# ReLU and row sum of 32 x 512 x 1024: who waits for the last store, and what closes the program

## Chip, core and metric

One core of a Trainium2 chip runs the kernel. The metric is the time of one execution on the device, in microseconds (us). Five engines have instruction streams of their own and meet only at semaphores: PE (TensorE), ACT (ScalarE), DVE (VectorE), POOL (GpSimd) and SP (SyncE). SP computes nothing here; it issues the transfers and waits.

## What is computed

```python
def reference(x):                      # x: 32 x 512 x 1024, float32
    relu_x = np.maximum(x, 0)
    return np.sum(relu_x, axis=-1)     # 32 x 512, float32
```

There are 16,384 rows of 1024 numbers. Each is clamped at zero and summed. 67.1 MB are read and 64 KB are written.

## The kernel before

**Tiling.** The 128 partitions hold 128 rows at a time, so each partition has 128 rows to sum. They come in seven blocks of 16 rows per partition (8 MB a block, `TWO`, `ACT`, `DVE`, lines 14 to 16) in three buffers `io`, and an eighth block that arrives in shrinking pieces: 8, 4, 2 and 1 rows (`TAIL`, line 18), and then the last row in four column pieces of 244 to 268 numbers (`PIECES`, line 19).

**Work on a block.** In the first six blocks ACT clamps groups of rows in place (`clamp`, line 112), and DVE sums them (`total`, line 120). In the sixth block ACT also does two rows by itself (`act_row`, line 127: clamp and sum in one instruction). The seventh block is shared row by row: nine rows on ACT and seven on DVE (`dve_row`, line 137). The eighth is shared in turns. The sums stand in one tile, `res`. The last row's four parts are summed on DVE one after the other; the last of them (line 205) also adds in the three sums before it.

**Transfers.** All transfers are issued on SP: 15 loads (line 94) and three stores of `res` (line 105). The first load is moved ahead of the program's opening barrier (`issue_ahead_of_the_barrier`, `EARLY`). A load into a used buffer waits until DVE is done with the block that was in it. The third store, 1 KB, holds the last two rows of each partition and waits for the last DVE instruction (lines 104, 105, 215). Every store adds 16 to the semaphore `stored` when it lands, so all three have landed when it is 48.

**Order and semaphores.** Nothing is scheduled by the framework: each engine runs its instructions in the order of the code, and semaphores are written by hand (`Semaphores`, line 47). There are 18 of them, which the trace numbers 99 to 116; 116 is `stored`.

**The opening barrier.** The framework opens the program with an all-engine barrier (line 259 in the profile). ACT, DVE, PE and SP each run a drain that adds one to a gather semaphore (96), then an event instruction that waits for a release semaphore (97) and takes one from it. POOL runs a drain, an event that waits until 96 is 4 and takes 4 off, and an event that adds 4 to 97. The trace of before has a record of each of these instructions.

**The closing block.** The framework also makes a closing block. As it makes it, it holds this, in order: a drain on SP; an all-engine barrier of the same 11 instructions as the opening one; on POOL a drain and a range clear that sets semaphores 99 to 116 to zero; and a second all-engine barrier of 11 instructions. The kernel before empties this block (line 41) and puts three things in: on POOL a wait for `stored` (line 42), POOL's drain of the clear, and the range clear (`semaphore_clear`, line 219, returns these two). In the trace the wait is not an instruction of its own: POOL's drain at line 29 carries it. PE, ACT, DVE and SP have nothing in the block.

**After the kernel** the runtime runs its own closing barriers and clears; they carry no line of the kernel and are not in the span, but the trace has their semaphore updates. [...]

Of the kernel before, what the change touches and what calls it, by code (L numbers as in the profile page):

```python
# [23 lines left out]
def kernel(tc: tile.TileContext, x: bass.AP, out: bass.AP):  # L24
    nc = tc.nc
    sems = Semaphores(tc)

    tc.close()
    tc.compile()
    nc.cur_bb = nc.bb_map[tc.start_bb_name]  # L30
    body = nc.cur_bb.bb.instructions
    ends = list(body)
    body.clear()
    n_stores = relu_sum(nc, sems, x, out)
    body.extend(ends)


    nc.cur_bb = nc.bb_map[tc.start_bb_name + "_end"]
    body = nc.cur_bb.bb.instructions
    clear = semaphore_clear(body)  # L40
    body.clear()
    nc.gpsimd.wait_ge(sems.stored, 16 * n_stores)
    body.extend(clear)
    issue_ahead_of_the_barrier(tc, EARLY)


# [169 lines left out]
    return n_store  # L216


def semaphore_clear(instructions):

    pool = [i for i in instructions if i.engine == mybir.EngineType.Pool]
    at = next(
        n for n, i in enumerate(pool) if getattr(i, "is_reset_sema", False)
    )
    return pool[at : at + 2]


def issue_ahead_of_the_barrier(tc: tile.TileContext, n_loads: int):


    SP = mybir.EngineType.SP
    blocks = tc.nc.main_func.blocks
    opening = blocks[0].instructions
    body = next(b for b in blocks if b.name == tc.start_bb_name).instructions
    loads = [i for i in body if i.engine == SP][:n_loads]
    for i in loads:
        assert isinstance(i, mybir.InstDMACopy)
        body.remove(i)
    at = next(
        n  # L240
        for n, i in enumerate(opening)
        if i.engine == SP and isinstance(i, mybir.InstDrain)
    )
    opening[at:at] = loads
# [30 lines left out]
```

## Time and profile before

| | us |
|---|---|
| median of 3 runs (161.95, 162.01, 162.01) | 162.01 |
| the profiled execution's own time | 161.95 |
| its span, from the kernel's first instruction to its last | 160.064 |
| lies around the span | 1.89 |
| DVE busy | 117.7 (74%) |
| ACT busy | 104.2 (65%) |
| POOL busy | 0.2 |
| mean rate of the transfers over the span | 420 GB/s |

Times in the profile count from the start of the span. A view prints microseconds with two digits or fewer; the trace under it has nanoseconds for the start and length of every instruction, and the time of every semaphore update. A letter q behind an engine (SPq, POOLq) stands for its sequencer: waits, drains, events and the issue of a transfer are not counted as busy time, but they have records. A record starts when the instruction's wait is over, so a wait is seen as the gap in front of it.

### The profile page before, as it was taken

The page shows a single profiled execution, that of the slowest core. Times are in us where ns is not written, and L with a number is a line of the kernel's source. Part 1 is how long each engine was busy: PE and PEld are TensorE (multiplying, and loading weights), DVE is VectorE, ACT ScalarE, POOL GpSimd, SP SyncE. Part 2 cuts the span into 40 slices and gives each one's busy share as a digit, 9 for nine tenths or more (in the row PEclk, how much of TensorE's full clock was granted, in tenths as well). Part 3 has the DMA queues.
Part 4 walks back from the last instruction along what each step waited for, and adds up shares of the span by engine and source line. Part 5 has one row for each costly group of instructions (what it writes and reads, how often), then busy time and mean ns, then how long its engine had stood idle before and what let it go on. Part 6 is the DMA issues. An engine that isn't in the chain of part 4 may idle for free.

```text
span 160.1 us, 133 instructions
## 1 busy us (share of the span) xinstructions
DVE 117.7 (74%) x43; ACT 104.2 (65%) x50; POOL 0.2 (0%) x4
## 2 busy tenths in 40 slices
DVE  0000000009999499994999999999999999999994
ACT  3000059990799708995099942999239992599993
POOL 0000000000000000000000000000000000000000
DMA  7996996996996996997998999979969969999993
GB/s 262 524 524 262 524 524 262 524 524 262 524 508 278 524 508 278 524 475 311 524 409 377 524 393 393 524 328 459 524 278 508 524 262 524 393 393 422 409 400 96
DMA packets 2592, 67.18 MB, mean 420 GB/s; under 512 B 672, under 2 KB 1184, under 8 KB 1312
## 3 DMA queue, kind: packets, MB, share of 16 engines
q1 hardware_dynamic: 2592, 67.18, 98.0%
HBM read 67.11 MB, written 0.07 MB: 420 GB/s over the span
## 4 chain that ended last, share of the span: by engine, by line
DMA 43%; DVE 33%; ACT 17%; another core or an unknown queue 3%; SPq 1%; issue 0%
DVE res L120 32%; DMA io<-in_x_dram 25%; DMA piece<-in_x_dram 18%; ACT io L112 17%; SPq L94 1%; DVE piece L137 1%; DVE piece L205 0%
## 5 line engine op out<-in xcount | busy, mean ns | idle before, releaser
L120 DVE TENSOR_REDUCE res<-io 128x8 f32<-128x8192 f32 (+2 forms) x9 | 101.1, 11287 | 40.0 <-ACT io L112 40.0
L112 ACT ACTIVATE io<-io 128x8192 f32<-128x8192 f32 (+2 forms) x9 | 81.7, 9110 | 47.1 <-DMA io<-in_x_dram 47.1
L127 ACT ACTIVATE io<-io 128x1024 f32<-128x1024 f32 x20 | 20.9, 1043 | 5.4 <-DMA io<-in_x_dram 5.3
L137 DVE TENSOR_SCALAR_CACHE_REDUCE io<-io 128x1024 f32<-128x1024 f32 x13 | 15.0, 1214 | 0.2
L127 ACT ACTIVATION_READ_ACCUMULATOR io<-io 128x1 f32 x20 | 3.7, 187 | 0.0
L112 ACT ACT_TABLE_LOAD x1 | 1.3, 1283 | 0.8 <-PEq L259 0.8
L137 DVE TENSOR_SCALAR_CACHE_REDUCE piece<-piece 128x244 f32<-128x244 f32 (+2 forms) x3 | 1.2, 416 | 0.4 <-DMA piece<-in_x_dram 0.4
L137 DVE DVE_READ_ACCUMULATOR io<-io 128x1 f32 x13 | 1.1, 82 | 0.0
L205 DVE TENSOR_SCALAR_CACHE_REDUCE piece<-piece 128x271 f32<-128x271 f32 x1 | 0.4, 435 | 0.0
L137 DVE DVE_READ_ACCUMULATOR piece<-piece 128x1 f32 x3 | 0.3, 84 | 0.0
L259 POOL MEMSET const-bfloat16-1.0<- 128x1 bf16 x1 | 0.1, 101 | 0.0
L259 POOL MEMSET const-uint8-127<- 128x1 uint8 x1 | 0.1, 101 | 0.0
L259 POOL MEMSET const-float32-0.0<- 128x1 f32 x1 | 0.1, 98 | 0.2 <-issue 0.2
L259 POOL MEMSET const-float32-1.0<- 128x1 f32 x1 | 0.1, 98 | 0.0
L205 DVE DVE_READ_ACCUMULATOR piece<-piece 128x1 f32 x1 | 0.1, 82 | 0.0
## 6 DMA issues: line engine op xcount, KB each, us to landing
io<-in_x_dram SPq DMA_DIRECT2D x1, 4096.0 KB, 21.6
io<-in_x_dram SPq DMA_DIRECT2D x1, 2048.0 KB, 26.1
io<-in_x_dram SPq DMA_DIRECT2D x1, 1024.0 KB, 28.1
io<-in_x_dram SPq DMA_DIRECT2D x1, 512.0 KB, 28.9
piece<-in_x_dram SPq DMA_DIRECT2D x1, 134.0 KB, 28.5
piece<-in_x_dram SPq DMA_DIRECT2D x1, 130.0 KB, 28.6
piece<-in_x_dram SPq DMA_DIRECT2D x1, 126.0 KB, 28.7
piece<-in_x_dram SPq DMA_DIRECT2D x1, 122.0 KB, 28.8
```

Of the source, the lines that this page charges most:

```text
L94: dma = nc.sync.dma_start(out=dst, in_=src)
L112: i = nc.scalar.activation(out=ap, in_=ap, func=RELU)
L120: nc.vector.tensor_reduce(out=res[:, m : m + n], in_=ap, axis=mybir.AxisListType.X, op=ADD).wait_op(sems.act, n_act, "sem-ge").then_inc(se ...
L127: i = nc.scalar.activation(out=ap, in_=ap, func=RELU, accum_out=res[:, m : m + 1])
L137: i = nc.vector.tensor_scalar(out=ap, in0=ap, scalar1=0.0, scalar2=None, op0=MAX, op1=ADD, accum_out=accum_out,)
L205: nc.vector.tensor_scalar(out=last[:, :], in0=last[:, :], scalar1=0.0, scalar2=None, op0=MAX, op1=ADD, accum_out=res[:, NT - 1 : NT],).wai ...
L259: nc = _bacc.Bacc("TRN2", target_bir_lowering=False, num_devices=1)
```

## The change

The closing block is no longer cut down. It keeps all that the framework put there, and a wait for `stored` on SP is put in front of it. The function that picked POOL's two instructions is gone.

```diff
     nc.cur_bb = nc.bb_map[tc.start_bb_name + "_end"]
     body = nc.cur_bb.bb.instructions
-    clear = semaphore_clear(body)
+    ends = list(body)
     body.clear()
-    nc.gpsimd.wait_ge(sems.stored, 16 * n_stores)
-    body.extend(clear)
+    nc.sync.wait_ge(sems.stored, 16 * n_stores)
+    body.extend(ends)
     issue_ahead_of_the_barrier(tc, EARLY)
...
-def semaphore_clear(instructions):
-
-    pool = [i for i in instructions if i.engine == mybir.EngineType.Pool]
-    at = next(
-        n for n, i in enumerate(pool) if getattr(i, "is_reset_sema", False)
-    )
-    return pool[at : at + 2]
```

The closing block then reads, engine by engine:

```text
SP     [wait stored >= 48] drain; drain, 96 += 1; wait 97 >= 1, 97 -= 1; drain, 96 += 1; wait 97 >= 1, 97 -= 1
ACT, DVE, PE                      drain, 96 += 1; wait 97 >= 1, 97 -= 1; drain, 96 += 1; wait 97 >= 1, 97 -= 1
POOL   drain; wait 96 >= 4, 96 -= 4; 97 += 4; drain; clear 99..116; drain; wait 96 >= 4, 96 -= 4; 97 += 4
```

Each drain that adds to 96 also waits until 97 is 0. Loads, compute and stores are the same in both kernels.

## Prediction

> **What bounds the kernel now.** I read the page's head and chain first, to see what sets the end.
>
> ```profile
> span 160.1 us, 133 instructions
> ...
> DMA 43%; DVE 33%; ACT 17%; another core or an unknown queue 3%; SPq 1%; issue 0%
> ```
>
> The loads and the compute fed by them make the time, and the diff touches none of them. So only the part behind the last sum can move. Next, the chain in order of time and the timeline of the last 2 us (start, length, what):
>
> ```profile
> 127.86 28.83 DMA piece<-in_x_dram
> 156.69 0.02 issue
> 156.72 1.18 DVE piece L137 x6
> 157.90 0.03 issue
> 157.92 0.44 DVE piece L205 x2
> ```
>
> ```profile
> 158.28 0.08 DVE L205 DVE_READ_ACCUMULATOR piece<-piece 128x1 f32 x1
> 158.39 0.33 SPq L105 DMA_DIRECT2D out_dram<-res  x1
> ```
>
> The chain view stops at the last compute instruction, DVE's at 158.36, yet the span runs to 160.06. The 1.70 us between are the last store and what waits for it. The instructions of line 29 (POOL's closing ones) are seen only when that line is asked for:
>
> ```profile
> L29 POOLq DRAIN  x1: 88/88/88, 159.8 to 159.8; - x1
> L29 POOLq EVENT_SEMAPHORE_RANGE_CLEAR  x1: 136/136/136, 159.9 to 159.9; - x1
> ```
>
> In nanoseconds: the store is issued from 158.394, its last landing is at 159.787, POOL's drain starts at 159.811 (0.024 later), and the clear ends at 160.064, the end of the span. From the drain's start to the clear's end it is 0.088 + 0.029 gap + 0.136 = **0.253 us**. This stretch is on the path, and here the change puts its instructions.
>
> **Behind the span.** The trace's updates of semaphore 2 show the runtime's closing chain: 1.003, 157.597, 160.590, 160.634, 160.657, 160.754, 160.794, 160.828, 160.874. Its gaps tell who is who. PE left the opening barrier at 0.771 and adds first (0.232 later); ACT's last instruction ends at 157.489 and it adds second (0.108 later); the third update has to be POOL's, since DVE (158.36) and SP (158.73) were done long before: it comes 0.526 after the clear. The rest follows in hops of 0.023 to 0.097. So POOL, and POOL alone, holds back the end of the program now: what moves the end of POOL's work moves the time by as much, unless another engine becomes later in this chain.
>
> **The price list.** The barrier that the change adds twice at the end has already run once, at the opening (line 259; smallest/median/largest ns, first to last start):
>
> ```profile
> L259 POOLq EVENT_SEMAPHORE  x2: 17/17/17, 0.6 to 0.7; - x2
> L259 DVEq DRAIN  x1: 10/10/10, 0.1 to 0.1; - x1
> L259 ACTq DRAIN  x1: 8/8/8, 0.1 to 0.1; - x1
> ...
> L259 POOLq DRAIN  x1: 179/179/179, 0.3 to 0.3; - x1
> L259 PEldq DRAIN  x1: 8/8/8, 0.3 to 0.3; - x1
> ...
> L259 SPq DRAIN  x1: 132/132/132, 0.4 to 0.4; - x1
> ...
> L259 PEldq EVENT_SEMAPHORE  x1: 51/51/51, 0.7 to 0.7; - x1
> ```
>
> In nanoseconds, SP arrives last: a transfer's issue ends 0.049 before its drain, the drain runs 0.431 to 0.563, POOL's two events start at 0.589 and 0.667, the second ends at 0.684, and the four engines' events start at 0.709 to 0.720. PE's is the last to end, at 0.771.
>
> **The change, step by step, from the moment `stored` is 48.**
>
> 1. The wait moves from POOL to SP. Nothing is queued behind it but SP's closing instructions, for which the barrier waits. POOL started 0.024 after the last landing; SP's last issue started 0.017 after the DVE update that it waited for (158.377 to 158.394). I take no difference: 0.00.
> 2. SP's two drains. SP's only drain took 0.132, just after an issue; those of ACT, PE and DVE took 0.008 to 0.010. Here the first comes 1.0 us after SP's last issue and the second right after another drain. I take SP's own row for the first and DVE's for the second, with the gap of 0.049: 0.132 + 0.049 + 0.010 = **0.191** (ends: 0.046 with 0.008 twice and a gap of 0.03; 0.313 with 0.132 twice).
> 3. The first barrier's end, from the end of SP's drain to the end of POOL's release: 0.684 - 0.563 = **0.121**. ACT, DVE, PE and POOL come to it early (the latest, DVE, is done at 158.36, 1.4 us before), so their drains cost nothing; were SP not last, DVE's would cost 0.010.
> 4. POOL's clear drain and clear: a gap of 0.029 before, then the 0.253 that before pays too: **0.282**. The four engines leave the first barrier and arrive at the second meanwhile: out within 0.087 of POOL's release by the opening's rows, plus a drain of 0.008 to 0.132. That is 0.22 at most against 0.282, so POOL's clear hides it by 0.06; an engine that came later than that would add what it exceeds.
> 5. The second barrier on POOL: gap 0.029, drain 0.088 (line 29's row; ends 0.008 and 0.179), gap 0.029, then from event to event 0.078 and the last event's 0.017: **0.241**.
>
> Sum: 0.191 + 0.121 + 0.282 + 0.241 = 0.835 against 0.253 before, so POOL ends **0.58 us later**. The span grows by some 0.09 more, since PE's last event ends 0.087 after POOL's; the time doesn't, because PE has that much slack in the runtime's chain: its first hop would come 0.087 + 0.232 behind POOL's release, and two hops of 0.035 and 0.038 (the same hops of the runtime's last chain, 161.704, 161.738, 161.776) make it 0.39, while POOL itself takes 0.526.
>
> The profiled execution took 161.95, so the change makes it 161.95 + 0.58 = 162.53. The median of the runs shown is 0.06 above this execution; for the median I forecast **162.59**.
>
> [...] The runtime's own chain that runs last takes 162.061 - 161.704 = 0.357 here, from first update to last. [...]
>
> **Rivals.**
>
> *The tail is hidden (not slower).* POOL's 0.526 between the clear and its update in the runtime's chain is far more than PE's 0.232 or ACT's 0.108. If it belongs to the clear and runs on beside later instructions, the second barrier lies under it. It can shrink only until PE's and ACT's part of the chain is last: PE's release ends 0.087 after POOL's, then a tail like ACT's 0.108, then 0.073 of hops, 0.268 in all. From a POOL tail under 0.27 on, the saving is 0.526 - 0.268 = 0.26, and the change costs 0.58 - 0.26 = 0.32: 162.27, within 0.2%. For it: POOL's tail is the odd one out, and only POOL ran a clear. Against it: the clears are recorded as updates of 99 to 116 at 159.949 to 160.036, before the record ends, so nothing is seen to run on; and if POOL's sequencer is what is busy, the drain behind the clear has to wait for it just as well, which leaves the sum as it is.
>
> *The gaps are dearer.* No row shows POOL going from an event to a drain or from a clear to a drain. If these three gaps are like the 0.078 between its events (+0.15), both SP drains take 0.132 (+0.12), POOL's drain takes the opening's 0.179 (+0.09), and the wait stands by itself as an event on SP (0.017 and a gap of 0.045, +0.06), it is 0.58 + 0.42 = 1.00: 161.95 + 1.00 + 0.06 = 163.01. For it: drains differ by a factor of 20 between engines here. Against it: they all have to go this way.
>
> *The change doesn't do what it says.* The time could stay at 162.01 if the runtime's chain, not the kernel's end, were the limit. The updates speak against that: third to seventh come in hops right behind POOL.
>
> **Numbers.** Forecast (0.45 to 0.80 more) 0.73; dear gaps (above that) 0.13; hidden tail 0.11; nothing, or a gain by something that no row shows, 0.03 (0.01 and 0.02). About 0.2% (0.32 us) is what a measurement of this kernel can tell from no change. Slower by more 0.86, within it 0.12, faster 0.02. The range takes in the hidden tail's 162.27 with some of the cheap drains (step 2 at its low end is 0.145 less, so 162.13 with both; I stop at 162.20) and ends at the dear case's 163.0.
>
> **What the trace would show.** Step 1: SP's first drain starts within 0.03 of the last landing. Steps 2 to 5: some 23 instructions more in the closing block, with SP's two drains summing to about 0.14, POOL's clear some 0.34 later behind the landing than now, and POOL's last event 0.58 later. The span is near 160.73. In semaphore 2 the first three updates stand close together, with the third still some 0.5 behind POOL's release; if it stands at 0.27, the hidden tail was right. I'm wrong if the last load or the last sum moves, or if an engine other than SP arrives last at the first barrier.

## The result, and the profile after

| | before | changed kernel |
|---|---|---|
| median | 161.98 us (4 runs, 161.94 to 162.01) | 162.59 us (4 runs, 162.49 to 162.68) |
| ratio | 1 | 1.0038, 95% interval 1.0020 to 1.0055 |
| profiled execution: time, span | 161.95, 160.064 | 162.68, 160.736 |
| instructions in the profile | 133 | 156 |

The change makes the kernel slower by 0.61 us. The forecast was 162.59.

The page's head and chain of the changed kernel:

```profile
span 160.7 us, 156 instructions
...
DMA 43%; DVE 33%; ACT 17%; another core or an unknown queue 3%; SPq 1%; issue 0%; DVEq 0%
```

The shares are those of before: loads and compute still make the time. The timeline of its last microseconds (start, length, what):

```profile
158.06 0.43 DVE L204 TENSOR_SCALAR_CACHE_REDUCE piece<-piece 128x271 f32<-128x271 f32 x1
158.43 0.08 DVE L204 DVE_READ_ACCUMULATOR piece<-piece 128x1 f32 x1
158.54 0.33 SPq L104 DMA_DIRECT2D out_dram<-res  x1
```

The last sum and the last store are as before, but 0.14 later. The rest is in the closing block, line 29 of the changed kernel (smallest/median/largest ns, first to last start):

```profile
L29 POOLq EVENT_SEMAPHORE  x4: 17/17/17, 160.0 to 160.6; - x4
L29 POOLq DRAIN  x3: 34/41/82, 0.7 to 160.5; - x3
L29 SPq DRAIN  x3: 7/7/7, 160.0 to 160.3; - x3
L29 PEldq DRAIN  x2: 8/8/8, 0.9 to 160.3; - x2
L29 ACTq DRAIN  x2: 14/595/1176, 156.5 to 160.3; - x2
...
L29 PEldq EVENT_SEMAPHORE  x2: 51/51/51, 160.2 to 160.7; - x2
L29 POOLq EVENT_SEMAPHORE_RANGE_CLEAR  x1: 136/136/136, 160.3 to 160.3; - x1
```

Two things are to be seen here. First, 23 more records, as the diff says. Second, SP's drains take 0.007 us each, not the 0.132 of the opening. ACT's first drain is 1.176 long, but it starts at 156.496, under ACT's own last instructions, and ends at 157.672, 2.26 ahead of the last landing; it costs nothing on the path.

The path in nanoseconds, from the record starts and ends of the trace: last landing 159.936; SP's drain with the wait 159.952; SP's second drain ends 160.014; POOL's release of the first barrier ends 160.135; POOL's clear drain runs 160.199 to 160.281, the clear 160.310 to 160.446; POOL's second release ends 160.648; PE's last event ends 160.736. The updates of semaphore 2 behind the kernel start at 160.971, 161.005, 161.210 (POOL's) and 161.254.

An update has a semaphore and a time in the trace, and neither an engine nor a line; "the runtime's" stands for what comes behind the kernel's last instruction, and the engines are read from the times. As in before, the first update of the closing chain comes some 0.23 behind PE's last event (0.235) and the third some 0.5 behind POOL's last instruction (0.562). Nine more updates of semaphore 2 follow in both profiles, the last chain: in before at 161.704, 161.738, 161.776, 161.820, 161.844, 161.942, 161.980, 162.014 and 162.061, in the changed kernel at 162.281, 162.316, 162.354, 162.398, 162.421, 162.520, 162.558, 162.714 and 162.761. A step is the time from one update to the next and is numbered by the update that it ends with.

I cut the end of every profiled execution into three stretches: K (the kernel's) from the last landing to the end of POOL's last instruction; P (POOL's tail) from there to POOL's update of semaphore 2; R (the rest) from that update to the end of the time. The trace marks neither end of the measured time; I count it from the start of the span, so R holds all of the time that lies outside the span behind that update or ahead of the first instruction, and a part of R that no update shows can't be placed. What comes ahead of the last landing is left out, since the landing itself moves between executions (159.68 to 159.99 in the profiles of this study). Differences are against before.

| | K | P | R | K+P+R less before's | change of the medians |
|---|---|---|---|---|---|
| before | 0.277 | 0.526 | 1.360 | 0 | 0 |
| changed kernel | 0.712 | 0.562 | 1.470 | +0.58 | +0.61 |

### The profile page after: what moved, and what is told of

The parts are those of the page before. It is cut to its first block, busy times and chain, and to the rows that moved or that the text cites. A ratio compares the mean times of both kernels' runs of the same rounds, so it can differ in the third digit from the quotient of the medians.

```text
span 160.7 us, 156 instructions
## 1 busy us (share of the span) xinstructions
DVE 117.7 (73%) x43; ACT 104.2 (65%) x50; POOL 0.2 (0%) x4
## 4 chain that ended last, share of the span: by engine, by line
DMA 43%; DVE 33%; ACT 17%; another core or an unknown queue 3%; SPq 1%; issue 0%; DVEq 0%
DVE res L119 32%; DMA io<-in_x_dram 25%; DMA piece<-in_x_dram 18%; ACT io L111 17%; SPq L93 1%; DVE piece L136 1%; DVE piece L204 0%; DVEq L29 0%
```

## The experiments

Theory A is the prediction's: only what stands behind the last landing on POOL's path, and what its tail and the runtime add to it, costs time. The rivals are that the longer program also delays the transfers (B), that POOL's tail belongs to the clear and hides later work (C), and, found on the way, that the number of instructions in the block lengthens the runtime's closing wherever they run (D).

**1. The changed kernel once more.** No edit.

> The changed kernel once more, unchanged, to see what of its 0.61 us is the same in every execution. In its first profile POOL's work behind the last landing took 0.44 us more than before, its tail 0.04 more, and the last landing itself came 0.15 later because one of the 16 DMA engines started its first load 0.30 late. Theory A (the closing block is all of the cost; the late engine is chance): the closing block from SP's drain to POOL's last event is again 0.70 us, but the last landing of the first load moves between profiles, and the time is 0.48 over before, with single runs 0.1 to either side. Theory B (the longer program also delays the transfers): the first load's last landing is again near 21.99 and the time is 0.61 over before.

Measured: 162.57 against 162.02, ratio 1.0035 (1.0023 to 1.0048). The first load's last landing came at 21.783 (21.992 in the first profile, 21.821 in before), the last store's at 159.792. So the late landing was chance, and theory B falls. What makes a landing late isn't shown, and the late start that the expectation names isn't shown to do it: the last of the first load's 16 first packets started at 1.405 in before, at 1.897 in the first profile and at 2.041 here, and here the landing was early. Stretches K and P are the same to the nanosecond, 0.712 and 0.562, and R is 1.474. The first profile's time holds 0.15 of chance, the median 162.59 less of it.

**2. The first barrier alone.** In this and the next three, `first`, `clear` and `second` are the closing block's 12, 2 and 11 instructions, as in experiments 10 and 11; the lines that split it are left out.

```diff
-    body.extend(ends)
+    body.extend(first + clear)
```

> SP waits, then the first barrier and POOL's clear; the second barrier is left out. Theory A (each instruction on POOL's path adds its own time): 0.06 for SP's drains, 0.12 to POOL's release, 0.31 to the clear's end, against 0.25 before: 0.24 us over before. Theory C (POOL's 0.53 us between its last instruction and its step in the runtime's chain belongs to the clear and can run beside a barrier): here nothing follows the clear, so 0.24 as well, and all of the rest is in the second barrier, which would then cost little.

Measured: 162.51 against 162.02, ratio 1.0030 (1.0019 to 1.0042): 0.49, twice the 0.24 expected. Its line 29:

```profile
L29 POOLq DRAIN  x2: 41/62/82, 0.7 to 160.2; - x2
L29 SPq DRAIN  x2: 7/7/7, 159.9 to 160.0; - x2
L29 POOLq EVENT_SEMAPHORE  x2: 17/17/17, 160.0 to 160.1; - x2
...
L29 POOLq EVENT_SEMAPHORE_RANGE_CLEAR  x1: 136/136/136, 160.3 to 160.3; - x1
```

The kernel's part is as theory A has it: K is 0.510, 0.233 over before, and P is 0.526. The other 0.24 is in R, 1.595, outside the kernel's span (0.17 on average over all six runs, see the table at the end).

**3. The second barrier alone.** POOL waits and clears as before.

```diff
-    nc.sync.wait_ge(sems.stored, 16 * n_stores)
-    body.extend(ends)
+    nc.gpsimd.wait_ge(sems.stored, 16 * n_stores)
+    body.extend(clear + second)
```

> POOL waits for the stores and clears as before; behind it the second barrier alone. Theory A: 0.20 us of POOL's drain and two events, and a tail 0.04 longer: 0.24 over before. Theory C: the barrier lies in POOL's tail, at most 0.05 over before. A third reading, that the cost is the wait's move to SP and the first barrier: 0.00 here.

Measured: 162.45 against 162.02, ratio 1.0029 (1.0019 to 1.0040): 0.43. K is 0.480 (+0.20), P 0.561 (+0.035), R 1.595 (+0.24). The barrier isn't hidden in POOL's tail; the tail comes whole behind it, and theory C falls here. R is again 0.24 longer in the profile (0.18 on average over eight runs). Two drains of line 29 are worth a look:

```profile
L29 POOLq DRAIN  x2: 34/61/88, 159.9 to 160.2; - x2
...
L29 SPq DRAIN  x1: 129/129/129, 158.9 to 158.9; - x1
```

POOL's drain behind the clear takes 0.034, and SP's, which here comes 0.05 behind the issue of the last store, takes 0.129.

**4. Both barriers, the wait on POOL between them.**

```diff
-    nc.sync.wait_ge(sems.stored, 16 * n_stores)
-    body.extend(ends)
+    body.extend(first)
+    nc.gpsimd.wait_ge(sems.stored, 16 * n_stores)
+    body.extend(clear + second)
```

> Both barriers stay, but the wait for the stores is on POOL behind the first barrier, so all engines pass the first barrier while the last store is under way. Theory A (only what stands behind the wait costs): the same as with the second barrier alone, 0.24 over before. If instead the number of barriers or instructions costs, wherever they stand: 0.48 as in the changed kernel.

Measured: 162.41 against 162.02, ratio 1.0024 (1.0012 to 1.0036): 0.39. K is 0.474 (+0.20) and P 0.561, as with the second barrier alone: the first barrier, done by 159.29 while the store was under way, costs nothing there (K was 0.480 without it). R is 1.468, which is the changed kernel's and not that of the two kernels with one barrier.

So R depends on something that the kernels with both barriers share. In their traces the eighth of the nine steps in the runtime's last chain takes 0.16 where before has 0.034, and the time ends 0.08 ahead of the last update; in before it ends 0.11 ahead of it; in the two kernels with one barrier the chain is as in before, but the time ends 0.12 behind the last update. So of R's growth the updates show 0.08 with both barriers and nothing with one; the 0.23 there may lie behind the last update or ahead of the span.

**5. Both barriers ahead of the wait.**

```diff
-    nc.sync.wait_ge(sems.stored, 16 * n_stores)
-    body.extend(ends)
+    body.extend(first + second)
+    nc.gpsimd.wait_ge(sems.stored, 16 * n_stores)
+    body.extend(clear)
```

> Both barriers stand ahead of POOL's wait for the stores, so all their instructions run while the last store is under way; behind the wait there are POOL's drain and clear alone, as before. It has the changed kernel's instructions but for the engine that waits. In the runs so far the closing block on POOL grew by 0.20 to 0.44 us, while the times grew by 0.39 to 0.55: some 0.1 to 0.2 us come behind the kernel, in the runtime's own closing. Theory A (only the path behind the last landing costs): same as before, within 0.1. Theory D (more instructions in the block, wherever they run, lengthen the runtime's closing by 0.1 to 0.2 us): 0.1 to 0.2 over before.

Measured: 162.17 against 162.08, ratio 1.0007 (0.9998 to 1.0016). K is 0.270 and P 0.527, as before. Its line 29 shows the second barrier over before the store had landed (last landing 159.832):

```profile
L29 POOLq EVENT_SEMAPHORE  x4: 17/17/17, 159.0 to 159.4; - x4
L29 POOLq DRAIN  x3: 34/41/82, 0.7 to 159.9; - x3
...
L29 PEldq EVENT_SEMAPHORE  x2: 51/51/51, 159.2 to 159.5; - x2
L29 POOLq EVENT_SEMAPHORE_RANGE_CLEAR  x1: 136/136/136, 160.0 to 160.0; - x1
```

R is nevertheless 1.481, with the eighth step at 0.166. The median can't tell this 0.12 from nothing, but the trace can: the step is slow although every barrier was long over. So can the time less the span, which is 0.11 longer on average (11 runs against 27 of before, standard error 0.01). That speaks for theory D.

**6. The kernel before, as an experiment.** No edit.

> The kernel before, unchanged, measured as if it were a changed one, for a second profile of it and for what an equal kernel gives: 0.00 with an interval of some 0.1% to either side, single runs 0.1 to 0.2 apart, the first load's last landing anywhere from 21.8 to 22.0, and behind the clear the same 0.526 on POOL and 0.36 in the runtime's last chain.

Measured: 162.06 against 162.08, ratio 1.0003 (0.9992 to 1.0015). K, P and R are 0.276, 0.527 and 1.352. Single runs of before lie between 161.84 and 162.76 in this study, but these stretches repeat within 0.01 in the two profiles.

**7. Four more instructions on ACT.** Against before; the drains run when ACT is done, and nothing waits for them.

```diff
+    for engine, n in [("scalar", 4)]:
+        for _ in range(n):
+            getattr(nc, engine).drain()
     nc.gpsimd.wait_ge(sems.stored, 16 * n_stores)
```

> The kernel before with four more drains on ACT in the closing block; they run at 157.5 us, while DVE and the stores are at work. The changed kernel has four more instructions on ACT than before. With both barriers, even when both ran early, the eighth step of the runtime's last chain took 0.16 us instead of 0.03, the pause before that chain 0.79 instead of 0.83, and the time stood 0.03 further from the last update: 0.11 us in all, all behind the kernel. Theory D (the runtime's closing follows the kernel's instructions in each engine's stream, and the step that is late is ACT's, so four more on ACT alone do it): hop 0.16 and 0.1 over before. If another engine's added instructions do it, or the barriers' waits and not their number: hop 0.034 and the time of before.

Measured: 162.10 against 162.00, ratio 1.0009 (1.0000 to 1.0017). Where the drains ran:

```profile
L44 ACTq DRAIN  x4: 8/11/1176, 156.3 to 157.6; - x4
```

They are over 2 us ahead of the last landing, and K and P are before's (0.276, 0.527). The eighth step of the last chain takes 0.166 and R is 1.520, 0.16 more. Theory D with ACT as the engine foretold it. Which engine makes the eighth step isn't shown.

**8. Two more on ACT.**

```diff
+    for engine, n in [("scalar", 2)]:
```

> The same with two drains on ACT, as many instructions as one barrier adds there. With one barrier the runtime's chains were as before, but the time stood 0.12 behind the last update instead of 0.11 ahead of it: 0.23 more. Theory D with ACT as the engine: no slow hop, the time 0.12 behind the last update and 0.23 over before. Otherwise as before.

Measured: 162.26 against 162.00, ratio 1.0017 (1.0008 to 1.0025). The eighth step is 0.035, and the time ends 0.11 behind the last update: R is 1.575, 0.22 more, as expected. None of this 0.22 is between two updates, so the trace doesn't place it. In these two profiles two instructions more cost more than four; over 11 runs each it is 0.19 against 0.16, with standard errors of 0.02 and 0.01, so that order isn't shown.

**9. The other engines' added instructions, without ACT's.**

```diff
+    for engine, n in [("tensor", 4), ("vector", 4), ("sync", 5), ("gpsimd", 6)]:
```

> The kernel before with the changed kernel's number of instructions on every engine but ACT: four drains more on PE, four on DVE, five on SP, six on POOL, all run ahead of the last landing (POOL's ahead of its wait). Theory D with ACT as the engine: as before, hop 0.034. If the number of instructions on another engine does it: hop 0.16 and 0.1 over before. If neither this nor the four on ACT does it, the cause isn't the number of instructions.

Measured: 162.00 against 162.00, ratio 1.0000 (0.9992 to 1.0009). The eighth step is 0.034. R is 1.312, 0.05 under before: the pause ahead of the last chain is 0.787 instead of 0.830, which the changed kernel shows as well (0.785). With the 0.16 of the four on ACT this makes 0.11, the changed kernel's growth of R to a hundredth.

**10. POOL waits and doesn't clear.** Against before; the range clear is left out.

```diff
-    body.extend(clear)
+    body.extend(clear[:1])
```

> As before, but POOL only waits for the stores with its drain; the range clear is left out, so the kernel leaves its semaphores as they are to the runtime's own closing, whose updates of 99 to 116 are in every trace. Theory A: 0.029 and 0.136 less on POOL, its tail stays at 0.53: 0.17 under before. Theory C (the tail belongs to the clear): tail 0.3 or less, 0.4 or more under before.

Measured: 161.91 against 162.08, ratio 0.9992 (0.9983 to 1.0001). K is 0.111, 0.166 less; P is 0.525. POOL's tail is the same with no clear in the program, so it isn't the clear's.

**11. SP waits, and nothing else.** Against the changed kernel; both barriers and the clear are left out.

```diff
-    body.extend(ends)
+    body.extend(first[:1])
```

> SP's first drain waits for the stores, and nothing else is in the closing block: no barrier and no clear of the semaphores, which is left to the runtime's closing. SP is the fifth in the runtime's chain, so POOL, PE, ACT and DVE would have added before it. The fifth update came at 160.657 in the kernel before. Theory A (what ends last in the runtime's chain sets the time): SP's tail is between ACT's 0.11 and POOL's 0.53, so the fifth update comes at 159.95 to 160.36 and the time is 0.3 to 0.7 under before. If the runtime's closing waits on something else behind the landing, the time stays.

Measured: 161.27 against 162.08, ratio 0.9946 (0.9933 to 0.9958): 0.81 faster than before, a little more than expected, and the fastest of all. Its whole closing block is one record:

```profile
L29 SPq DRAIN  x1: 7/7/7, 160.0 to 160.0; - x1
```

The closing chain's third update (POOL's, by the order of before) comes at 157.883, 2.106 ahead of the last landing (159.989 in this profile), where before has it 0.803 behind the landing; the fourth (DVE's) comes at 158.720 and the fifth (SP's) at 160.133, 0.144 behind the landing. In before the fifth came 0.870 behind the landing and 0.067 behind the third, though SP's last instruction had ended at 158.726: POOL's tail stood ahead of it. That is 0.73 of the gain; what comes behind the fifth update is 0.05 shorter as well (1.247 against 1.293).

All kernels in the three stretches (the last three columns as differences to before). "P+R, all runs" doesn't rest on one profile: it is the time less the span, averaged over all runs of the kernel (6 to 12) less that of before (16 to 29); where the second barrier comes last, the 0.09 by which PE's last event ends behind POOL's is added. Spans are listed to 0.1, and the standard error is 0.01 to 0.02.

| kernel | K | P | R | sum | P+R, all runs | medians |
|---|---|---|---|---|---|---|
| changed kernel, again | 0.712 | 0.562 | 1.474 | +0.59 | +0.14 | +0.55 |
| first barrier alone | 0.510 | 0.526 | 1.595 | +0.47 | +0.17 | +0.49 |
| second barrier alone | 0.480 | 0.561 | 1.595 | +0.47 | +0.21 | +0.43 |
| both, wait on POOL between | 0.474 | 0.561 | 1.468 | +0.34 | +0.16 | +0.39 |
| both ahead of the wait | 0.270 | 0.527 | 1.481 | +0.12 | +0.11 | +0.09 |
| four more on ACT | 0.276 | 0.527 | 1.520 | +0.16 | +0.16 | +0.10 |
| two more on ACT | 0.277 | 0.526 | 1.575 | +0.22 | +0.19 | +0.26 |
| the others' instructions | 0.271 | 0.527 | 1.312 | -0.05 | -0.06 | 0.00 |
| no clear | 0.111 | 0.525 | 1.363 | -0.16 | -0.02 | -0.17 |

The averages agree with the profiles' P and R within 0.03, except with one barrier, where the profiles show 0.06 to 0.07 more.

## Why the prediction was right, and where not

The path was right. The total was right to 0.01 us by luck: the closing block cost 0.14 less than forecast, and POOL's tail and R, which the forecast held fixed, cost 0.15 more.

- *Step 1, the wait moves to SP, 0.00:* SP's drain started 0.016 behind the last landing, POOL's had started 0.024 behind it. Right.
- *Step 2, SP's two drains, 0.191:* from SP's first drain to the end of its second it was 0.062. **This step failed.** I gave SP's drain the 0.132 of the opening. The experiments show what that row was: where SP's drain comes right behind the issue of the last store, as in experiments 3 to 5, it takes 0.129 to 0.131; a microsecond later, or behind another drain, it takes 0.007. The low end (0.046) was the near one.
- *Step 3, the first barrier's end, 0.121:* 160.014 to 160.135, 0.121. Right to the nanosecond; its row was the same instructions on the same engines.
- *Step 4, 0.282:* 0.311. The gap from POOL's event to its drain was 0.064, not 0.029. The other engines' arrival at the second barrier was hidden, as forecast: PE's drain ended at 160.330, 0.12 ahead of the clear's end.
- *Step 5, 0.241:* 0.202, since POOL's drain behind the clear took 0.034 and not 0.088; the gap behind that drain was 0.044, not 0.029.
- *The sum:* from the start of the drain that carries the wait, POOL ended 0.443 us later than before instead of 0.58 (0.435 from the landing).
- *POOL's tail unchanged:* nearly. It is 0.562 behind an event and 0.526 behind a drain or a clear, so 0.036 more.
- *The rest behind POOL's update unchanged:* this assumption wasn't even named as a step, and it failed. R grew by 0.11, which replaced most of what I had priced too high; 0.08 of it lies between updates that the trace shows. Experiments 7 and 9 reproduce it with added drains that nothing waits for: +0.16 from four on ACT, -0.05 from the rest (+0.16 and -0.06 over all runs).

Of the rivals, the hidden tail needed a tail under 0.27; it was 0.562 in the changed kernel and 0.525 with no clear. Dear gaps didn't come either: two of the three gaps were wider (0.064 and 0.044 instead of 0.029), but the drains were cheaper. That rival was also priced 0.05 too high: its 0.078 runs from the start of one POOL event to the start of the next, and the gap between them is 0.061. That the kernel's end isn't the limit is refuted by experiments 10 and 11, where it moves the time down. Of the signs named, POOL's clear started 0.23 later behind the landing than before (forecast 0.34), SP's two drains summed to 0.014 (forecast 0.14), and POOL's last event ended 0.44 later behind the landing and not 0.58. The span of 160.74 met the forecast 160.73 only with the 0.15 of the late landing; in experiment 1 it was 160.59. One sign of being wrong showed too, the last sum 0.14 later, which experiment 1 puts down to chance.

A barrier costs tenths of a microsecond here, as the rows had it: the opening one takes 0.34 in before, from the start of SP's drain at 0.431 to the end of PE's event at 0.771, and the kernel's two closing barriers together put 0.435 on the path (K).

Left open: how more instructions on ACT make the time longer. In all 13 profiles the kind of delay goes with the number of instructions added to ACT (none: none; two: a time that ends behind the last update; four: a slow eighth step), and the size isn't in proportion (none 0, two 0.19, four 0.16 over all runs). Not tried: three or more than four instructions on ACT, and which of the other engines gives the 0.05 back.

## What to carry to other kernels

Find the engine that ends last in the closing and count only what stands behind its last wait: a barrier ahead of that wait cost nothing on that path (K 0.270 with both ahead, 0.277 in before), a barrier behind it 0.20 to 0.23 us. Its instructions aren't free for that: with both barriers ahead of the wait the time outside the span still grew by 0.11. Let an engine with a short way out wait for the last store: with SP waiting alone (its step comes 0.12 behind its last instruction, POOL's 0.53) and POOL done early, the kernel was 0.5% faster than before. Of these 0.81 us, 0.17 came from leaving out the clear with POOL still waiting (experiment 10). Both hold only if the semaphores are cleared behind the kernel; the trace of before has an update of each of 99 to 116 there, at 160.934 to 161.205, but not its value. For effects of a few tenths of a microsecond, compare stretches of the trace that begin at the last common event; K and P repeat within 0.01 us where single times differ by some tenths. A size that rests on one profile should be averaged over more runs, as R with one barrier shows.

## What the runs showed of the hardware

- Instructions that run early, wait for no other engine and are waited for by nobody still moved the time: two drains more on ACT cost 0.22 us in the profile and 0.19 on average over 11 runs, four 0.16 in both, all outside the kernel's span. With four, 0.13 of it is the eighth step of the last chain (0.166 against 0.034); with two, no update shows where it is.
- From an engine's last instruction to the update of the closing chain that I read as its own, where the update ahead of it had come earlier or there was none: ACT 0.11 and PE 0.23 us (before), SP 0.12 and DVE 0.15 (experiment 11), but POOL 0.53 behind a drain (experiment 10) or a clear (before) and 0.56 behind an event (changed kernel).
- An SP drain took 0.129 to 0.133 us within 0.05 us of the end of a transfer's issue and 0.007 otherwise. POOL's took 0.082 to 0.088 ahead of the clear, 0.034 behind it, and 0.034 as well in experiment 5, where it came behind an event.
- The last of 16 landings of the first load moved between 21.69 and 22.01 from one profile to the next, also between two profiles of one program (21.992 and 21.783), and the last store landed 137.93 to 138.01 later in 12 of the 13 profiles (138.10 in the other). Single runs of before differ by up to 0.9 us, but their time less span by 0.11 at most, so nearly all of this lies inside the span; that it is this landing in every run isn't shown.
